# A ninth seven-product pair in the down products of a float32 encoder trunk

## The chip, the cores and the metric

The kernel runs on one core of a Trainium2 chip. The core has TensorE (PE, matrix products), VectorE (DVE), ScalarE (ACT) and GpSimd (POOL), each working off its own list of instructions in order, and SyncE (SP), which issues DMAs. The engines wait for one another by semaphores. The metric is the device time of one launch in microseconds. In the profile PEld is the loading of a weight tile into PE, which lies beside the matmuls.

## The reference

Two layers work on 256 tokens of width 2048, all in float32. Layer 0 mixes tokens with a convolution module, layer 1 with multi-head latent attention; each is followed by the same MLP, on which the change bears:

```python
h = rms_norm(x, norm_mlp_g[layer])
x = x + jnp.square(jax.nn.relu(h @ w1)) @ w2      # w1: 2048 x 8192, w2: 8192 x 2048
...
return rms_norm(x, final_norm_g)
```

## The kernel before

**Products in halves.** A float32 value is used as a sum of two rounded ones, `hi` and `lo`. A weight tile of 1 MB (two or four blocks of 128 rows) is loaded by SP into one of three `raw` buffers; ACT copies it into `hi` (the copy rounds, L170 or L497), DVE forms `lo = raw - hi` (L174 or L498). A product is then three matmuls into the same PSUM bank: hi x hi, hi x lo, lo x hi (`mm3`, L203 to L205).

**The MLP.** `mlp` (L609) cuts the 8192 hidden columns into two halves (`hf`). In each half the *up product* (L640 to L687) makes 4096 hidden columns in eight groups of four blocks: PE's products with `w1` (L655, L656), then on ACT and DVE the sum, the squared ReLU and the scaling by `r2_row` (L673 to L677), and the split of the result into `hi` and `lo`. A group holds two *pairs* of 128-row blocks; a half has 16 pairs. The *down product* (L708 to L754) multiplies these 16 pairs by `w2` in two *sweeps*, `n = 0` and `n = 2`, each over two column blocks of 512. A pair, two token tiles and two column blocks make a 2 x 2 by 2 x 2 block product.

**Two ways to do a pair.** `Sums.plain` (L559) does it with eight products, 24 matmuls. `Sums.mixed` (L546) does it with seven products (Strassen's scheme in Winograd's form), 21 matmuls. Seven products need sums of weight blocks: `mixed_weights` (L490) splits b11, b21 and b22 (1024 and 512 columns), overwrites `raw` with four differences t1 to t4 (L505, 1024 columns; L506 and L507, 512 each), and splits those too (2 x 1024). They also need sums of the inputs, which `mixed_inputs` (L512) makes during the up product: seven blocks instead of four, so more memory. `MIXED` (L44) lists the pairs that are done so: eight of 16, seven in the last half of layer 1.

**Banks and the join.** A sweep uses eight PSUM banks: four sums `e[t][c]`, one for each token tile and column block, and four shared ones, u1, u6, u7, u5. `join` (L582) adds up the shared ones after the last mixed pair, while PE does the last plain pairs, and `put` (L575) adds the results to the residual `xs`: on DVE, or, where `by_dma` holds, by an adding DMA that POOL issues (L578). `by_dma` holds in both sweeps of the first half of each layer and in the first sweep of layer 1's second half, five sweeps in all. `close` (L595) then adds the four `e`.

**What sets the order.** The code names a sequence; a list scheduler of the tile framework turns it into one fixed order for each engine, by its own estimates of when operands and buffers will be free. So a change in buffers also changes the order. Within a sweep the code interleaves mixed pairs (M) and plain ones (P) by L713: the first sweep of eight was P P MM P MM P M P MM P M P [join] P, the second P M P M P MM P M P M P MM P [join] P. Buffers: three `raw`; six of `hi` and six of `lo` of 1024 columns (`WB`), one ring for all stages in `wpool`; four `v` tiles, used for the up product's results and as room for the join.

## Time and profile before

| | |
|---|---|
| median of 3 runs | 1934.01 us (1933.93 to 1934.53) |
| the profiled execution | 1934.31 us, its span in the trace 1932.5 us |
| granted TensorE clock | 0.999 |
| layer 0: up, down, up, down | from 300.3, 478.0, 641.4 and 819 us |
| layer 1: up, down, up, down | from 1241.3, 1419.2, 1582.4 and 1760 us, to 1925 us |
| ACT busy in these down products | 91 to 93 us each |
| POOL busy over the span | 249.0 us (13%) |

The page is one execution. A row of a group reads: line, engine, operation, what is written <- what is read, shape, count | busy us, mean ns of one | idle us before them and what ended it. A row of the timeline reads: start us, length, engine, line, operation; `x2` are two in a row, and brackets tell the idle time before and who ended it. Lengths of neighbouring instructions of one engine overlap a little, so what an instruction costs in a row of many is read from one start to the next. A row of stretches gives, after the length, the busy us of PE, PEld, DVE, ACT and POOL.

### The profile page before, as it was taken

The page shows a single profiled execution, that of the slowest core. Times are in us where ns is not written, and L with a number is a line of the kernel's source. Part 1 is how long each engine was busy: PE and PEld are TensorE (multiplying, and loading weights), DVE is VectorE, ACT ScalarE, POOL GpSimd, SP SyncE. Part 2 cuts the span into 40 slices and gives each one's busy share as a digit, 9 for nine tenths or more (in the row PEclk, how much of TensorE's full clock was granted, in tenths as well). Part 3 has the DMA queues.
Part 4 walks back from the last instruction along what each step waited for, and adds up shares of the span by engine and source line. Part 5 has one row for each costly group of instructions (what it writes and reads, how often), then busy time and mean ns, then how long its engine had stood idle before and what let it go on. Part 6 is the DMA issues. An engine that isn't in the chain of part 4 may idle for free.

```text
span 1932.5 us, 28477 instructions
## 1 busy us (share of the span) xinstructions
PE 1921.0 (99%) x10725; PEld 1681.5 (87%) x10725; DVE 1592.2 (82%) x2457; ACT 1095.6 (57%) x1636; POOL 249.0 (13%) x208
## 2 busy tenths in 40 slices
PE   9999999999999999999999999999999999999998
PEld 8999888888888888888898998888888888888887
DVE  7999988877999776799976766877789987678998
ACT  5667755554555545555576655555555554455554
POOL 6999200000010100000001420000000010000000
PEclk9999999999999999999999999999999999999999
DMA  7766456665585866655656545465646776665774
GB/s 230 214 183 189 153 189 206 193 194 177 175 251 194 263 195 187 194 174 196 217 176 175 142 134 192 155 216 186 188 162 225 222 248 212 191 196 175 231 219 150
DMA packets 230427, 375.50 MB, mean 194 GB/s; under 512 B 16392, under 2 KB 107792, under 8 KB 230032
## 3 DMA queue, kind: packets, MB, share of 16 engines
q1 hardware_dynamic: 224640, 363.28, 58.7%
q0 software_dynamic: 4320, 7.87, 2.2%
q10 hardware_dynamic: 1328, 2.52, 0.4%
q8 instruction: 84, 1.38, 0.3%
q14 instruction: 55, 0.45, 0.1%
HBM read 363.68 MB, written 2.10 MB: 189 GB/s over the span
## 4 chain that ended last, share of the span: by engine, by line
PE 97%; DVE 2%; DMA 0%; ACT 0%; issue 0%; ACTq 0%; DVEq 0%
PE acc L655 24%; PE acc L205 15%; PE acc L203 15%; PE acc L204 15%; PE acc L656 13%; PE acc L823 8%; PE acc L1287 2%; DVE sum L910 1%; DMA xs<-in_x 0%; PE acc L1535 0%; PE acc L1566 0%; PE acc L1565 0%; PE acc L1536 0%; PE acc L1564 0%; PE acc L1537 0%; PE tr L267 0%
## 5 line engine op out<-in xcount | busy, mean ns | idle before, releaser
L174 DVE TENSOR_TENSOR lo<-raw,hi 128x1024 fp32r<-128x1024 f32 (+2 forms) x509 | 602.2, 1197 | 232.3 <-ACT hi L170 226.6
L170 ACT ACTIVATE hi<-raw 128x1024 fp32r<-128x1024 f32 (+2 forms) x574 | 583.9, 1036 | 361.1 <-PE acc L655 203.7
L655 PE MATMUL acc<-xt,hi 128*128 128x512 f32 x2048 | 710.6, 390 | 0.0
L656 PE MATMUL acc<-xt,lo 128*128 128x256 f32 x2048 | 577.5, 282 | 0.0
L655 PEld LDWEIGHTS acc<-xt,hi 128*128 128x128 f32 x2048 | 384.3, 188 | 80.7
L656 PEld LDWEIGHTS acc<-xt,lo 128*128 128x128 f32 x2048 | 387.1, 189 | 0.2
L497 ACT ACTIVATE hi<-raw 128x1024 fp32r<-128x1024 f32 x248 | 228.7, 948 | 228.3 <-DVE raw L505 134.0
L498 DVE TENSOR_TENSOR lo<-raw,hi 128x1024 fp32r<-128x1024 f32 x248 | 263.9, 1087 | 27.6 <-ACT hi L497 22.5
L203 PE MATMUL acc<-hi,sh 128*128 128x512 f32 x514 | 200.1, 389 | 0.0
L205 PE MATMUL acc<-lo,sh 128*128 128x512 f32 x514 | 200.1, 389 | 0.0
L203 PE MATMUL acc<-hi,gh 128*128 128x512 f32 (+1 forms) x516 | 200.0, 388 | 0.0
L205 PE MATMUL acc<-lo,gh 128*128 128x512 f32 (+1 forms) x516 | 199.9, 387 | 0.0
L204 PE MATMUL acc<-hi,gl 128*128 128x512 f32 (+1 forms) x516 | 199.9, 387 | 0.0
L823 PE MATMUL acc<-xt,hi 128*128 128x256 f32 x1024 | 180.2, 281 | 0.3 <-ACT b L1106 0.2
L204 PE MATMUL acc<-hi,sl 128*128 128x512 f32 x450 | 175.1, 389 | 0.0
L578 POOL DMA_DIRECT2D xs<-v x30 | 26.5, 994 | 1136.4 <-DVE lo L174 703.2
L910 DVE SCALAR_TENSOR_TENSOR sum<-ub,w_dw,sum 128x256 f32<-128x256 f32 x409 | 164.3, 481 | 3.6 <-ACT sum L880 3.0
L174 POOL TENSOR_TENSOR lo<-raw,hi 128x1024 fp32r<-128x1024 f32 x65 | 155.0, 2410 | 17.3 <-ACT hi L170 17.3
L823 PEld LDWEIGHTS acc<-xt,hi 128*128 128x128 f32 x1024 | 154.8, 188 | 1.1 <-ACT xt L1090 0.6
L823 PE MATMUL acc<-xt,lo 128*128 128x256 f32 x512 | 139.2, 279 | 0.0
L205 PEld LDWEIGHTS acc<-lo,sh 128*128 128x128 f32 x514 | 96.5, 188 | 20.4 <-DVE lo L498 0.3
L204 PEld LDWEIGHTS acc<-hi,gl 128*128 128x128 f32 x516 | 96.9, 188 | 19.9
(314 smaller groups left out, 2531.3 us busy)
## 6 DMA issues: line engine op xcount, KB each, us to landing
raw<-in_mlp_w SPq DMA_DIRECT2D x255, 1024.0 KB, 5.5
raw<-in_conv_w_pw SPq DMA_DIRECT2D x62, 512.0 KB, 5.1
raw<-in_conv_w_pw SPq DMA_DIRECT2D x16, 1024.0 KB, 5.1
raw<-in_mla_w_o SPq DMA_DIRECT2D x16, 1024.0 KB, 5.7
raw<-in_mla_w_kv_up SPq DMA_DIRECT2D x32, 256.0 KB, 3.9
xs<-v POOLq DMA_DIRECT2D x30, 256.0 KB, 7.8
raw<-in_mla_w_in SPq DMA_DIRECT2D x8, 576.0 KB, 3.8
raw<-in_mla_w_in SPq DMA_DIRECT2D x4, 1024.0 KB
```

Source lines behind the costliest of these rows:

```text
L170: nc.scalar.activation(hi, raw[:, js, :], AF.Copy)
L174: eng.tensor_tensor(lo, raw, hi.bitcast(F32), op=ALU.subtract)
L203: nc.tensor.matmul(ps, sh, mh, start=start, stop=False)
L204: nc.tensor.matmul(ps, sl, mh, start=False, stop=False)
L205: nc.tensor.matmul(ps, sh, ml, start=False, stop=stop)
L497: nc.scalar.activation(hi, src, AF.Copy)
L498: nc.vector.tensor_tensor(lo, src, hi.bitcast(F32), op=ALU.subtract)
L655: nc.tensor.matmul(ps[b], wh[:, bs], xhl(k), start=k == 0, stop=False)
L656: nc.tensor.matmul(ps[b][:, :S], wl[:, bs], xh(k), start=False, stop=k == KC - 1)
L823: nc.tensor.matmul(pss[c][b][:, :S], w[i][:, bs], (xh, xl)[j](k), start=k == i + j == 0, stop=end and k == k0 + nk - 1 and (i, j) == terms ...
L910: nc.vector.scalar_tensor_tensor(out=out, in0=ubs[c][:, w : w + S], scalar=tap(c, w), in1=base, op0=ALU.mult, op1=ALU.add)
L1287: nc.tensor.matmul(ps2[b][t], x_kt(k, t), w[:, bs], start=k == g == i == 0, stop=k == KC - 1 and i == len(group) - 1,)
```

## The change

A ninth pair (pair 2) is done with seven products, in all four halves; the last half has eight instead of seven. To make room for its inputs, and for the way the lower halves are now made, several things change with it:

- `mixed_weights`: b21, b22 and b11 lie side by side in `raw` and are split at once, with 1536 columns (one ACT copy and one DVE difference in place of two each). The differences are formed in another order of blocks, with the same widths, and split in two steps of 1024.
- Split buffers: `hi` and `lo` of the MLP are of two kinds, `a` (two buffers of up to 1536 columns: the first half of a plain unit, the 1536 columns of a mixed one) and `b` (three of 1024). They and those of the other stages now come from a pool that each stage opens for itself.
- `mixed_inputs`: three blocks are split in one step.
- `join` uses three rooms, not four; the first shared sum goes to `xs` by a DVE addition, never by DMA. There are three `v` tiles; `r2_row` lies in `scratch`.
- The hidden results are kept in tiles by pair, with tiles of its own for pairs 2 and 3.

```diff
-MIXED = {(layer, half): (0, 1, 4, 5, 8, 9, 12) + (13,) * (layer + half < 2) for layer in range(2) for half in range(2)}
-N_MIXED = 4
+MIXED = {(layer, half): (0, 1, 2, 4, 5, 8, 9, 12) + (13,) * (layer + half < 2) for layer in range(2) for half in range(2)}
+SPLIT_BUFS = {"a": 2, "b": 3}
...
+    def open_halves(cx, name, kinds=False):
+        halves_of[:] = [cx.enter_context(tc.tile_pool(name=name, bufs=1, reuse_waits="tile"))]
+        two_kinds[0] = kinds
+
+    def in_halves(shape, kind=None):
+        kind = kind if two_kinds[0] else None
+        n = WB if kind is None else SPLIT_BUFS[kind]
+        return [halves_of[0].tile(shape, F32R, tag=c + (kind or ""), name=nm(c), bufs=n) for c in ("hi", "lo")]
...
-        hi = wpool.tile([P, nj // 2, cols], F32R, tag="hi", name=nm("hi"), bufs=WB)
-        lo = wpool.tile([P, nj // 2, cols], F32R, tag="lo", name=nm("lo"), bufs=WB)
+        hi, lo = in_halves([P, nj // 2, cols], "ab"[h])
...
-        b11, b21 = halves(raw[:, :, :NB])
-        (b22,) = halves(raw[:, 1:2, NB:])
-        top = raw[:, 0, :].rearrange("p (c n) -> p c n", c=2)
-        low = raw[:, 1, :].rearrange("p (c n) -> p c n", c=2)
-        nc.vector.tensor_tensor(top, raw[:, :, NB:], top, op=ALU.subtract)
-        nc.vector.tensor_tensor(low[:, 1, :], low[:, 1, :], top[:, 0, :], op=ALU.subtract)
-        nc.vector.tensor_tensor(low[:, 0, :], low[:, 0, :], low[:, 1, :], op=ALU.subtract)
-        t1, t3 = halves(top)
-        t4, t2 = halves(low)
+        r = raw.rearrange("p j (c n) -> p (j c) n", c=2)
+        h1, l1 = in_halves([P, 3, NB], "a")
+        nc.scalar.activation(h1, r[:, :3, :], AF.Copy)
+        nc.vector.tensor_tensor(l1, r[:, :3, :], h1.bitcast(F32), op=ALU.subtract)
+        nc.vector.tensor_tensor(
+            r[:, 2:4, :], r[:, 3:4, :].broadcast_to([P, 2, NB]), r[:, 2:0:-1, :], op=ALU.subtract
+        )
+        nc.vector.tensor_tensor(r[:, 1, :], r[:, 1, :], r[:, 2, :], op=ALU.subtract)
+        nc.vector.tensor_tensor(r[:, 0, :], r[:, 0, :], r[:, 1, :], op=ALU.subtract)
+        b21, b22, b11 = ((h1[:, i, :], l1[:, i, :]) for i in range(3))
+        t = []
+        for i in (2, 0):
+            h2, l2 = in_halves([P, 2, NB], "b")
+            nc.scalar.activation(h2, r[:, i : i + 2, :], AF.Copy)
+            nc.vector.tensor_tensor(l2, r[:, i : i + 2, :], h2.bitcast(F32), op=ALU.subtract)
+            t += [(h2[:, j, :], l2[:, j, :]) for j in range(2)]
+        t1, t3, t4, t2 = t
...
-        halves(a[:, 0:1, :], 0, 1)
-        halves(a[:, 2:4, :], 1, 2)
+        halves(a[:, 0:3, :], 0, 3)
...
-            a, b, c, d = (room() for _ in range(4))
+            a, c, d = (room() for _ in range(3))
             nc.scalar.activation(a, u1, AF.Copy)
-            self.put(0, 0, a if self.by_dma else u1)
-            nc.vector.tensor_tensor(b, u6, a, op=ALU.add)
-            nc.vector.tensor_tensor(c, u7, b, op=ALU.add)
+            x = self.place(0, 0)
+            nc.vector.tensor_tensor(x, u1, x, op=ALU.add)
+            nc.vector.tensor_tensor(a, u6, a, op=ALU.add)
+            nc.vector.tensor_tensor(c, u7, a, op=ALU.add)
             nc.vector.tensor_tensor(d, u5, c, op=ALU.add)
-            nc.vector.tensor_tensor(b, u5, b, op=ALU.add)
-            for (t, n), o in (((1, 0), c), ((1, 1), d), ((0, 1), b)):
+            nc.vector.tensor_tensor(a, u5, a, op=ALU.add)
+            for (t, n), o in (((1, 0), c), ((1, 1), d), ((0, 1), a)):
                 self.put(t, n, o)
...
+            open_halves(cx, f"halves{layer}", kinds=True)
...
-            r2_row = mp.tile([P, S], F32, name=nm("r2_row"))
+            r2_row = scratch[:, :S]
...
-                return mp.tile([P, 2, S], F32, tag="v", name=nm("v"), bufs=4)
+                return mp.tile([P, 2, S], F32, tag="v", name=nm("v"), bufs=3)
```

The scheduler gives DVE another order. In the rows below the line numbers are those of each kernel: after the change L508 is the 1536-column lower half of a mixed pair, L509 the 1024-column difference, L512 and L513 the two of 512, L519 the lower halves of 1024, L185 those of a plain pair.

First place, DVE in the first sweep of layer 0's first down product, the end of a group of two mixed pairs and a plain one. Before, from the second mixed pair on:

```order
L498 TENSOR_TENSOR lo_5710<-raw_5707,hi_5709 128x1024
L498 TENSOR_TENSOR lo_5714<-raw_5707,hi_5713 128x512
L505 TENSOR_TENSOR raw_5707<-raw_5707 128x1024
L506 TENSOR_TENSOR raw_5707<-raw_5707 128x512
L507 TENSOR_TENSOR raw_5707<-raw_5707 128x512
L498 TENSOR_TENSOR lo_5721<-raw_5707,hi_5720 128x1024
L498 TENSOR_TENSOR lo_5725<-raw_5707,hi_5724 128x1024
L174 TENSOR_TENSOR lo_5752<-raw_5749,hi_5751 128x1024
L174 TENSOR_TENSOR lo_5756<-raw_5749,hi_5755 128x1024
```

After, from the third difference of the first mixed pair (`raw_5693`) on; `raw_5731` is the second, `raw_5769` the plain one:

```order
L513 TENSOR_TENSOR raw_5693<-raw_5693 128x512
L519 TENSOR_TENSOR lo_5703<-raw_5693,hi_5702 128x1024
L508 TENSOR_TENSOR lo_5734<-raw_5731,hi_5733 128x1536
L519 TENSOR_TENSOR lo_5707<-raw_5693,hi_5706 128x1024
L509 TENSOR_TENSOR raw_5731<-raw_5731 128x1024
L185 TENSOR_TENSOR lo_5772<-raw_5769,hi_5771 128x1024
L512 TENSOR_TENSOR raw_5731<-raw_5731 128x512
L519 TENSOR_TENSOR lo_5741<-raw_5731,hi_5740 128x1024
L513 TENSOR_TENSOR raw_5731<-raw_5731 128x512
L519 TENSOR_TENSOR lo_5745<-raw_5731,hi_5744 128x1024
L185 TENSOR_TENSOR lo_5776<-raw_5769,hi_5775 128x1024
```

What a pair's weights need was one block of rows; now the pairs are interleaved, and the last lower half of the second mixed pair follows directly on the last difference.

Second place, DVE at the end of the same sweep: the join, the closing additions (L601 before, L613 after) and the first splits of the next sweep. Before:

```order
L589 TENSOR_TENSOR v_6055<-acc_5477,v_6054 128x512
L174 TENSOR_TENSOR lo_6119<-raw_6116,hi_6118 128x1024
L590 TENSOR_TENSOR v_6056<-acc_5478,v_6055 128x512
L591 TENSOR_TENSOR v_6054<-acc_5478,v_6054 128x512
L174 TENSOR_TENSOR lo_6123<-raw_6116,hi_6122 128x1024
L498 TENSOR_TENSOR lo_6153<-raw_6150,hi_6152 128x1024
L498 TENSOR_TENSOR lo_6157<-raw_6150,hi_6156 128x512
L505 TENSOR_TENSOR raw_6150<-raw_6150 128x1024
L601 TENSOR_TENSOR xs<-acc_5471,xs 128x512
L601 TENSOR_TENSOR xs<-acc_5473,xs 128x512
```

After:

```order
L185 TENSOR_TENSOR lo_5996<-raw_5989,hi_5995 128x1024
L600 TENSOR_TENSOR v_6023<-acc_5474,v_6023 128x512
L185 TENSOR_TENSOR lo_6038<-raw_6035,hi_6037 128x1024
L601 TENSOR_TENSOR v_6024<-acc_5475,v_6023 128x512
L185 TENSOR_TENSOR lo_6042<-raw_6035,hi_6041 128x1024
L602 TENSOR_TENSOR v_6025<-acc_5476,v_6024 128x512
L603 TENSOR_TENSOR v_6023<-acc_5476,v_6023 128x512
L613 TENSOR_TENSOR xs<-acc_5469,xs 128x512
L613 TENSOR_TENSOR xs<-acc_5471,xs 128x512
L185 TENSOR_TENSOR lo_6088<-raw_6085,hi_6087 128x1024
L185 TENSOR_TENSOR lo_6092<-raw_6085,hi_6091 128x1024
L508 TENSOR_TENSOR lo_6122<-raw_6119,hi_6121 128x1536
```

The sum `c` (L589 before, `v_6024` of L601 after) and the closing addition to the same place (the second L601, the second L613) were nine rows apart with the next sweep's first splits between them; now the addition is five rows on, and the next sweep's first splits stand behind it.

Third place, DVE where the convolution module ends (residual additions L388 before, L399 after; transpositions L334, L345) and the MLP of layer 0 begins. Before:

```order
L174 TENSOR_TENSOR lo_3852<-raw_3845,hi_3851 128x1024
L174 TENSOR_TENSOR lo_3896<-raw_3893,hi_3895 128x1024
L388 TENSOR_TENSOR xs<-acc_3612,xs 128x512
L388 TENSOR_TENSOR xs<-acc_3613,xs 128x512
L334 STREAM_TRANSPOSE ca<-xs 32x2x4x32 x12
L174 TENSOR_TENSOR lo_3900<-raw_3893,hi_3899 128x1024
```

After, where `raw_3803` is the MLP's first unit:

```order
L399 TENSOR_TENSOR xs<-acc_3615,xs 128x512
L399 TENSOR_TENSOR xs<-acc_3616,xs 128x512
L345 STREAM_TRANSPOSE ca<-xs 32x2x4x32
L185 TENSOR_TENSOR lo_3806<-raw_3803,hi_3805 128x1024
L345 STREAM_TRANSPOSE ca<-xs 32x2x4x32 x2
L185 TENSOR_TENSOR lo_3810<-raw_3803,hi_3809 128x1024
```

Five splits of the MLP's first units stood ahead of the additions; now all stand behind them.

More of the change, by code (lines that the diff above doesn't have):

```diff
@@ L114, in trunk_kernel @@
     psum, psum_cx = {}, [ExitStack()]
+    halves_of, two_kinds = [], [False]
+    def open_halves(cx, name, kinds=False):
[5 more added lines that the diff above has]
+        return [halves_of[0].tile(shape, F32R, tag=c + (kind or ""), name=nm(c), bufs=n) for c in ("hi", "lo")]
     def repool(name, **banks):
@@ L490, in mixed_weights @@
     def mixed_weights(raw):
-        def halves(src):
-            hi = wpool.tile(list(src.shape), F32R, tag="hi", name=nm("hi"), bufs=WB)
-            lo = wpool.tile(list(src.shape), F32R, tag="lo", name=nm("lo"), bufs=WB)
-            nc.scalar.activation(hi, src, AF.Copy)
-            nc.vector.tensor_tensor(lo, src, hi.bitcast(F32), op=ALU.subtract)
-            return [(hi[:, i, :], lo[:, i, :]) for i in range(src.shape[1])]
-        b11, b21 = halves(raw[:, :, :NB])
-        (b22,) = halves(raw[:, 1:2, NB:])
-        top = raw[:, 0, :].rearrange("p (c n) -> p c n", c=2)
-        low = raw[:, 1, :].rearrange("p (c n) -> p c n", c=2)
-        nc.vector.tensor_tensor(top, raw[:, :, NB:], top, op=ALU.subtract)
-        nc.vector.tensor_tensor(low[:, 1, :], low[:, 1, :], top[:, 0, :], op=ALU.subtract)
-        nc.vector.tensor_tensor(low[:, 0, :], low[:, 0, :], low[:, 1, :], op=ALU.subtract)
-        t1, t3 = halves(top)
-        t4, t2 = halves(low)
+        r = raw.rearrange("p j (c n) -> p (j c) n", c=2)
[15 more added lines that the diff above has]
+        t1, t3, t4, t2 = t
         return b11, b21, b22, t1, t2, t3, t4
@@ L521, in mixed_inputs @@
         a = v.rearrange("p k (t n) -> p (k t) n", t=T)
-        a11, a21, a12, a22 = (a[:, i, :] for i in range(4))
-        halves(a[:, 0:1, :], 0, 1)
-        halves(a[:, 2:4, :], 1, 2)
+        a12, a22, a11, a21 = (a[:, i, :] for i in range(4))
+        halves(a[:, 0:3, :], 0, 3)
         nc.vector.tensor_tensor(a22, a21, a22, op=ALU.add)
-        nc.vector.tensor_tensor(a21, a11, a21, op=ALU.subtract)
+        nc.vector.tensor_tensor(a21, a21, a11, op=ALU.subtract)
         nc.vector.tensor_tensor(a11, a22, a11, op=ALU.subtract)
@@ L550, in mixed @@
             work = [
-                (u1, 0, b11), (u5, 6, t1), (u7, 4, t3), (u6, 3, t2),
-                (self.e[0][0], 1, b21), (self.e[0][1], 5, b22), (self.e[1][0], 2, t4),
+                (u1, 2, b11), (u5, 4, t1), (u7, 6, t3), (u6, 5, t2),
+                (self.e[0][0], 0, b21), (self.e[0][1], 3, b22), (self.e[1][0], 1, t4),
             ]
@@ L638, in mlp @@
                 plain = [g for g in range(ng) if g not in mixed]
-                gs = {}
+                fs = {}
                 for g in range(ng):
@@ L662, in mlp @@
                         beside = None
-                    if g in mixed or g in plain[len(plain) + len(mixed) - N_MIXED :]:
-                        shape = [P, 2, 7, P] if g in mixed else [P, 4, S]
-                        gs[g] = [mp.tile(shape, F32R, tag=f"s{c}", name=nm(f"s{c}"), bufs=N_MIXED) for c in "hl"]
-                    else:
-                        gs[g] = [mp.tile([P, 4, S], F32R, tag=f"g{c}", name=nm(f"g{c}"), bufs=ng - N_MIXED) for c in "hl"]
-                    gh, gl = gs[g]
+                    both = [2 * g, 2 * g + 1]
+                    if g % 2 == 0:
+                        tiles = [mp.tile([P, 2, 7, P], F32R, tag=f"s{c}", name=nm(f"s{c}"), bufs=ng // 2) for c in "hl"]
+                        for b2, p in enumerate(both):
+                            fs[p] = [a[:, b2] for a in tiles]
+                    elif g == 1:
+                        fs[2] = [mp.tile([P, 7, P], F32R, tag=f"o{c}", name=nm(f"o{c}")) for c in "hl"]
+                        fs[3] = [mp.tile([P, 2 * T, P], F32R, tag=f"p{c}", name=nm(f"p{c}")) for c in "hl"]
+                    else:
+                        tiles = [mp.tile([P, 2, 2 * T, P], F32R, tag=f"g{c}", name=nm(f"g{c}"), bufs=ng // 2 - 1) for c in "hl"]
+                        for b2, p in enumerate(both):
+                            fs[p] = [a[:, b2] for a in tiles]
                     for b2 in range(2):
@@ L677, in mlp @@
                         nc.vector.tensor_tensor(v, v, row, op=ALU.mult)
+                        h, l = fs[2 * g + b2]
                         if 2 * g + b2 in ms:
-                            mixed_inputs(v, gh[:, b2], gl[:, b2])
+                            mixed_inputs(v, h, l)
                             continue
-                        if g in mixed:
-                            v = v.rearrange("p k (t n) -> p (k t) n", t=T)
-                            h, l = gh[:, b2, : 2 * T, :], gl[:, b2, : 2 * T, :]
-                        else:
-                            h, l = (a[:, 2 * b2 : 2 * b2 + 2, :] for a in (gh, gl))
+                        v = v.rearrange("p k (t n) -> p (k t) n", t=T)
+                        h, l = h[:, : 2 * T, :], l[:, : 2 * T, :]
                         nc.scalar.activation(h, v, AF.Copy)
@@ L692, in at @@
                     def at(k, t):
-                        a = gs[k // 4][i]
-                        if k // 4 in mixed:
-                            return a[:, k % 4 // 2, k % 2 * T + t, :]
-                        return a[:, k % 4, t * P : (t + 1) * P]
+                        return fs[k // 2][i][:, k % 2 * T + t, :]
                     return at
@@ L703, in mixed_quad @@
                 def mixed_quad(sums, i):
-                    g, b = divmod(ms[i], 2)
-                    sums.mixed(w, k_lo + 4 * g + 2 * b, gs[g][0][:, b], gs[g][1][:, b], i == len(ms) - 1)
+                    sums.mixed(w, k_lo + 2 * ms[i], *fs[ms[i]], i == len(ms) - 1)
                 split_end = last and finish is not None
@@ L758, in trunk_kernel @@
     with ExitStack() as cx:
+        open_halves(cx, "halvesc")
         cv = cx.enter_context(tc.tile_pool(name="cv", bufs=1, reuse_waits="tile"))
@@ L1309, in rotary_tables @@
     def rotary_tables(pool):
-        place = pool.tile([P, 2, S], F32, tag="v", name=nm("v"), bufs=4).rearrange("p a n -> p (a n)")
+        place = pool.tile([P, 2, S], F32, tag="v", name=nm("v"), bufs=3).rearrange("p a n -> p (a n)")
         at = [0]
@@ L1370, in trunk_kernel @@
     with ExitStack() as cx:
+        open_halves(cx, "halvesa")
         at = cx.enter_context(tc.tile_pool(name="at", bufs=1, reuse_waits="tile"))
```

## The prediction

> **What bounds the kernel now.** I read the page's first two parts, then the busy times by stage, then the waits of PE, then PE and DVE instruction by instruction inside one down product.

> ```profile
> span 1932.5 us, 28477 instructions
> PE 1921.0 (99%) x10725; PEld 1681.5 (87%) x10725; DVE 1592.2 (82%) x2457; ACT 1095.6 (57%) x1636; POOL 249.0 (13%) x208
> ...
> PE acc L1001 <- POOL ident masks.py:199: 1.6, 1, 1.6
> PE acc L1061 <- DVE y L225: 0.6, 1, 0.6
> ...
> 300.30:478.00 177.70, 177.70 (x1027) 157.51 (x1026) 139.11 (x242) 95.47 (x140) 0.00 (x0) 1.00 0.60 190
> 478.00:641.40 163.40, 163.40 (x723) 135.32 (x722) 152.59 (x164) 92.70 (x104) 8.91 (x10) 1.00 0.65 209
> 819.00:980.00 161.00, 161.00 (x713) 133.05 (x712) 153.80 (x170) 91.14 (x109) 0.25 (x2) 1.00 0.57 190
> 1419.20:1582.40 163.20, 163.20 (x722) 135.12 (x721) 152.94 (x163) 92.68 (x104) 8.76 (x10) 1.00 0.65 209
> 1760.00:1925.00 165.00, 164.73 (x739) 136.68 (x737) 151.28 (x179) 91.60 (x116) 5.26 (x6) 1.00 0.61 198
> ```

> The last four rows are the four down products (busy us of PE, PEld, DVE, ACT and POOL after the length). PE is never idle there, and no wait of PE over 0.6 us lies outside the start. But DVE is busy 152.6 of 163.4 us: the stage that the change touches has two engines near their limit. What a matmul costs is read from starts, since the 0.39 us shown is pipelined:

> ```profile
> 640.13 0.39 PE L204 MATMUL acc<-hi,gl 128*128 128x512 f32 x1
> 640.36 0.39 PE L205 MATMUL acc<-lo,gh 128*128 128x512 f32 x1
> 640.58 0.39 PE L203 MATMUL acc<-hi,gh 128*128 128x512 f32 x1
> ```

> They start 0.22 to 0.23 us apart, and 163.4 / 723 is 0.226; I use 0.227. A plain pair (P, 24 matmuls) is 5.45 us of PE, a seven-product pair (M, 21) is 4.77.

> DVE in the first sweep of the first down product:

> ```profile
> 488.07 2.96 DVE L498 TENSOR_TENSOR lo<-raw,hi 128x1024 fp32r<-128x1024 f32 x3 [1.21 <-ACT hi L497]
> ...
> 498.24 1.82 DVE L498 TENSOR_TENSOR lo<-raw,hi 128x1024 fp32r<-128x1024 f32 x2
> ...
> 514.03 1.82 DVE L498 TENSOR_TENSOR lo<-raw,hi 128x1024 fp32r<-128x1024 f32 x2
> 515.77 1.22 DVE L505 TENSOR_TENSOR raw<-raw 128x1024 f32<-128x1024 f32 x1
> 517.02 0.69 DVE L506 TENSOR_TENSOR raw<-raw 128x512 f32<-128x512 f32 x1
> 517.75 0.69 DVE L507 TENSOR_TENSOR raw<-raw 128x512 f32<-128x512 f32 x1
> 518.36 2.52 DVE L498 TENSOR_TENSOR lo<-raw,hi 128x1024 fp32r<-128x1024 f32 x2
> 520.79 2.35 DVE L174 TENSOR_TENSOR lo<-raw,hi 128x1024 fp32r<-128x1024 f32 x2
> 523.07 1.82 DVE L498 TENSOR_TENSOR lo<-raw,hi 128x1024 fp32r<-128x1024 f32 x2
> ...
> 545.61 4.62 DVE L174 TENSOR_TENSOR lo<-raw,hi 128x1024 fp32r<-128x1024 f32 x4
> ```

> From 488 on DVE runs back to back. M takes it 520.79 - 514.03 = 6.76 us, P 2.28, M M P 514.03 - 498.24 = 15.79. So M is bound by DVE (6.76 against 4.77) and P by PE. The old sweep, P P MM P MM P M P MM P M P P, balances from its first M to the P behind its last: DVE 3 x 15.79 + 2 x 9.04 = 65.5, PE 3 x 14.98 + 2 x 10.22 = 65.4.

> **The change part by part.**

> *PE.* Eight sweeps lose three matmuls each: 24 x 0.227 = 5.4 us gained, if data is ready. The four up products prepare one more pair each; DVE has 177.7 - 139.1 = 38.6 us free there, which also covers the third tile in place of four, so 0. The loads keep their bytes.

> *Groups M M P.* The new first sweep is P P MMM P MM P MM P MM P P, the second P M P MM P MM P MM P MM P P: no M P is left in which DVE catches up. The new order of DVE (first place in the section on the change) is, for a group, S T t t s, then S' s T' P t' s t' s P', where S is the joined 1536-column difference, T the 1024-column one, t the 512-column ones, s a 1024-column lower half. Prices: 1024 columns (4.62 - 1.22) / 3 = 1.13; S between 1.13 + 0.54 (512 more columns by the two forms of L498 below) = 1.67 and the 1.74 of the two that it replaces, taken 1.67; T before a dependent t 1.25, t before t 0.73, t 0.61.

> ```profile
> L498 DVE TENSOR_TENSOR lo<-raw,hi 128x1024 fp32r<-128x1024 f32 x186 | 225.5, 1221 | 27.6 <-ACT hi L497 22.5 <-PE acc L205 0.6
> L498 DVE TENSOR_TENSOR lo<-raw,hi 128x512 fp32r<-128x512 f32 x62 | 42.4, 684 | 0.0
> L497 ACT ACTIVATE hi<-raw 128x1024 fp32r<-128x1024 f32 x186 | 195.0, 1058 | 222.3 <-DVE raw L505 134.0 <-DVE raw L507 34.5 <-PE acc L204 23.6
> L497 ACT ACTIVATE hi<-raw 128x512 fp32r<-128x512 f32 x62 | 38.4, 619 | 6.0 <-PE acc L204 5.9
> raw<-in_mlp_w SPq DMA_DIRECT2D x255, 1024.0 KB, 5.5
> ```

> S T t t s is 1.67 + 1.25 + 0.73 + 0.61 + 1.13 = 5.39. S' needs its ACT copy, 1.06 + 0.44 = 1.50 us, which ACT starts behind the copy for s, so at 5.50. Then S' 1.67, s 1.13, T' 1.13, P 1.13, t' 0.60, s 1.13, t' 0.69 bring it to 12.98. The last s needs the ACT copy of what that t' has just written; in the old order the other s stood in between, now nothing does: 1.21 idle, the price in the row at 488.07. With s and P', 1.13 each: 16.45 us, against PE's 66 x 0.227 = 14.98. There is a second limit: three buffers of loaded weights. The second M's is released by its last s, 15.3 us into the group; the load that follows takes 5.5, and its copy is wanted 4.0 us into the next group, at 20.4: 0.5 late. So a group takes 16.45 to 17.0 and PE loses 1.5 to 2.0; I take 1.8. The first group of a sweep is partly covered by DVE's lead: I take 0.5 between 0 and 1.8. Six sweeps of nine: 6 x (0.5 + 3 x 1.8) = 35. Layer 1's second half has eight: its first sweep three such groups, 3 us; its last, where units are half as wide (DVE 8 x 6.5 + 8 x 1.13 = 61 against PE (8 x 21 + 96) x 0.227 = 60), 4, between 0 and 8. Together 42, with ends of 12 (first two groups of each sweep covered, 1.0 for the others) and 65.

> *The join.* Two pieces of work change place (second place in the section on the change). Where sums go out by DMA, row (1,0) of the residual gets `c` by a POOL put, and then its plain sum by a DVE addition that must wait for that put.

> ```profile
> 550.87 0.69 DVE L589 TENSOR_TENSOR v<-acc,v 128x512 f32<-128x512 f32 x1
> ...
> 560.45 1.28 DVE L601 TENSOR_TENSOR xs<-acc,xs 128x512 f32<-128x512 f32 x2
> ...
> 552.12 0.87 POOL L578 DMA_DIRECT2D xs<-v  x1 [3.96 <-PE acc L205]
> ...
> xs<-v POOLq DMA_DIRECT2D x30, 256.0 KB, 7.8
> ...
> 642.10 0.69 DVE L601 TENSOR_TENSOR xs<-acc,xs 128x512 f32<-128x512 f32 x1 [0.50 <-DMA xs<-v]
> ...
> DMA to landing us min/median/max: 5.7/7.9/10.3
> ```

> Before, 9 us of other DVE work lie between `c` (ends 551.56) and the second L601 (561.05), POOL issues 0.56 us behind `c`, and a put lands 7.8 later (median of all; the last row is of the six around this sweep's end); even so the other sweep waits 0.50. Now only P, d, the last sum and one addition stand between, 1.13 + 3 x 0.6 = 2.9 us, so DVE waits 0.5 + 7.8 - 2.9 = 5.4 us, and behind it in DVE's order stand both halves of the next unit's weights. From the last s of the sweep: `c` ends after P, sum, P, sum = 3.5; addition possible at 11.8; next weights at 11.8 + 0.6 + 1.2 = 13.6. PE has then left 13 + 24 matmuls and some 0.7 us of handing over, 9.1. PE waits 4.5, at five ends of sweep: 22 us, with ends 0 (put landing in 2.9) and 30. The three temporaries make ACT's copies at the end wait for the same puts; they stand behind the next unit's copies and I charge nothing more. The added fourth addition (0.6) lies in the last s's wait; five puts fewer cost POOL nothing that anybody awaits.

> Where sums go by DVE (layer 0, second half), all four closing additions now stand ahead of the next weights, and the last needs the end of PE's last matmul: addition 0.6 + weights 1.22, some 2 us, twice: 4 (0 to 6).

> *Changes of stage.* Split buffers now belong to a pool of each stage. Entering layer 0's MLP, DVE used to split ahead of the residual additions, now behind (third place).

> ```profile
> 298.66 1.23 DVE L174 TENSOR_TENSOR lo<-raw,hi 128x1024 fp32r<-128x1024 f32 x1 [1.50 <-ACT hi L170]
> 299.83 1.37 DVE L388 TENSOR_TENSOR xs<-acc,xs 128x512 f32<-128x512 f32 x2
> 301.24 5.38 DVE L334 STREAM_TRANSPOSE ca<-xs 32x256 f32<-32x256 f32 x12
> ```

> The first lower half now follows two additions and one transposition (301.2 + 0.45) and ends at 302.9. PE comes to it at 300.3, where the first window above begins, and four matmuls with upper halves give it 0.9 us: 1.7 late. The same at layer 1's MLP; at attention, where three splits move behind the closing additions, 1.5: 5 in all (0 to 8).

> *Sum.* -5.4 + 42 + 22 + 4 + 5 = +68 us; the profiled execution took 1934.3 us, the median 1934.0, so 2002.

> [...]

> **Rivals.** 0.2% (3.9 us) is what a measurement here can tell from no change.
> - *Puts land in time*, groups slow: 2002 - 22 = 1980. For it: DVE's lag may delay PE too. Against: the rows at 552.12 and 642.10. [...] Chance 0.14.
> - *Groups keep up*: DVE idles less than the order says, and only join and stages cost: 1934 - 5.4 + 31 = 1960. For it: pure instruction time of a group is 15.1, almost PE's. Against: the 1.21 wait has no cover. Chance 0.15.
> - *Faster*: DVE's lead covers groups and turns, and PE alone counts: 1934 - 5.4 = 1929. It needs a group in 14.98 us, so the 1.21 wait gone and a load landing in 4, and a put in 2.9 us. Chance 0.06; no effect, 0.02.
> - *Weights late as well*: loads of 7 us in place of 5.5, as the three open units bunch them, and groups of 18: 24 x 1.2 more, 2031. Chance 0.05.

> **How the numbers follow.** The forecast has 0.58. The range leaves out the faster end and the far tail, 1950 to 2036. Faster 0.06, same 0.02, slower 0.92.

> **What would show it.** Right: PE about 8 x 3 matmuls shorter but with waits at L216 on DVE lo L519 and at ACT hi L518 in the down products, down stages of 175 us and more; DVE waiting 4 to 5 us on DMA xs<-v at the closing addition, five times; DVE's busy time in these stages above 158 us. Wrong: PE back to back in the down products, which would mean that DVE runs further ahead of PE than I count; or a put that lands within 3 us.

## The result, and the profile after

The changed kernel takes 2027.0 us (median of four runs, 2024.9 to 2028.9) against 1934.0 for the kernel before: a ratio of 1.048, 95% interval 1.046 to 1.050. It is slower, as forecast, but by 93 us and not by 68. The profiled execution has a span of 2024.4 us, 91.9 more than before. Page of the changed kernel:

```profile
span 2024.4 us, 28043 instructions
PE 1953.0 (96%) x10701; PEld 1673.4 (83%) x10701; DVE 1626.0 (80%) x2423; ACT 1099.9 (54%) x1557; POOL 244.5 (12%) x203
...
raw<-in_mlp_w SPq DMA_DIRECT2D x254, 1024.0 KB, 5.4
...
xs<-v POOLq DMA_DIRECT2D x25, 256.0 KB, 8.5
```

PE has 24 matmuls less, yet its busy time is 32 us longer: a matmul in front of a wait counts with its whole 0.39 us, and matmuls that start late (0.33 us apart behind a wait in place of 0.23) or run slowly (0.43 apart in the rows below) count as busy too. Below I therefore count from starts. The busy times by stage show where the time went (first up product, then the four down products; columns as in the prediction, with granted clock, DMA share and GB/s at the end):

```profile
300.20:479.90 179.70, 178.28 (x1027) 157.38 (x1026) 143.96 (x243) 97.98 (x136) 0.00 (x0) 1.00 0.61 194
479.90:665.30 185.40, 170.85 (x717) 133.64 (x715) 157.34 (x155) 92.37 (x88) 7.13 (x8) 0.98 0.57 179
847.10:1029.00 181.90, 170.73 (x732) 132.92 (x730) 165.85 (x172) 96.62 (x101) 0.25 (x2) 1.00 0.51 172
1469.30:1654.80 185.50, 170.06 (x716) 132.60 (x715) 157.33 (x155) 92.81 (x88) 6.96 (x8) 0.99 0.57 180
1834.90:2017.00 182.10, 171.84 (x734) 134.16 (x732) 159.74 (x177) 94.16 (x107) 4.39 (x5) 0.99 0.55 175
```

The down products take 182 to 185.5 us in place of 161 to 165 (the third row ends inside the start of attention), the up product 2 more. In them DVE is busier than before, yet idle for 16 to 28 us a stage, and the granted clock is 0.98 and 0.99 in three of the rows, where it was 1.00. What PE waits for, by line:

```profile
PE acc L214 <- ACT hi L518: 19.6, 26, 1.1
PE acc L216 <- DVE lo L185: 11.2, 3, 5.3
PE acc L214 <- ACT hi L507: 10.3, 16, 1.5
PE acc L669 <- DVE lo L185: 7.3, 4, 2.6
PE acc L216 <- DVE lo L519: 4.8, 7, 2.3
```

L507, L508, L518 and L519 are the weights of seven-product pairs, L185 those of plain pairs and of the up products. DVE's timeline shows one group M M P of the first sweep:

```profile
525.96 1.76 DVE L508 TENSOR_TENSOR lo<-raw,hi 128x1536 fp32r<-128x1536 f32 x1
...
532.16 1.76 DVE L508 TENSOR_TENSOR lo<-raw,hi 128x1536 fp32r<-128x1536 f32 x1 [0.59 <-ACT hi L507]
...
538.98 0.68 DVE L513 TENSOR_TENSOR raw<-raw 128x512 f32<-128x512 f32 x1
540.87 1.23 DVE L519 TENSOR_TENSOR lo<-raw,hi 128x1024 fp32r<-128x1024 f32 x1 [1.20 <-ACT hi L518]
542.01 1.22 DVE L185 TENSOR_TENSOR lo<-raw,hi 128x1024 fp32r<-128x1024 f32 x1
543.19 1.76 DVE L508 TENSOR_TENSOR lo<-raw,hi 128x1536 fp32r<-128x1536 f32 x1
```

The group takes 543.19 - 525.96 = 17.23 us, the one before it 16.63, with the uncovered wait of 1.20 where the forecast put it. And DVE at the end of that sweep, with its wait over all five such ends behind it:

```profile
562.44 0.68 DVE L601 TENSOR_TENSOR v<-acc,v 128x512 f32<-128x512 f32 x1
...
572.83 0.69 DVE L613 TENSOR_TENSOR xs<-acc,xs 128x512 f32<-128x512 f32 x1 [6.78 <-DMA xs<-v]
573.44 2.35 DVE L185 TENSOR_TENSOR lo<-raw,hi 128x1024 fp32r<-128x1024 f32 x2
```

```profile
DVE xs L613 <- DMA xs<-v: 24.0, 5, 6.8
```

The closing addition waits 6.78 us for the put of `c`, and the next weights stand behind it. What PE does then is new:

```profile
574.71 0.80 PE L216 MATMUL acc<-lo,ph 128*128 128x512 f32 x1 [5.27 <-DVE lo L185]
575.30 0.63 PE L214 MATMUL acc<-hi,ph 128*128 128x512 f32 x1
575.73 0.63 PE L215 MATMUL acc<-hi,pl 128*128 128x512 f32 x1
...
580.83 0.39 PE L215 MATMUL acc<-hi,pl 128*128 128x512 f32 x1
581.06 0.39 PE L216 MATMUL acc<-lo,ph 128*128 128x512 f32 x1
```

```profile
573.97:577.38 3.41, 2.67 (x6) 2.16 (x7) 3.41 (x3) 1.32 (x2) 1.45 (x2) 0.50 0.35 56
577.38:580.79 3.41, 3.41 (x9) 2.65 (x8) 2.05 (x3) 1.84 (x2) 0.32 (x1) 0.50 0.92 240
580.79:584.21 3.42, 3.42 (x16) 2.82 (x15) 2.81 (x4) 0.74 (x2) 0.00 (x0) 1.00 0.95 189
```

The last three rows are busy times by stretch: from 573.97 us on 6.8 us at a granted clock of 0.50, in which matmuls start 0.43 us apart and not 0.23, then 1.00 again. PE pays a second time for this wait: the 14 intervals from 574.71 to 580.83 us take 6.12 us, where 14 x 0.227 is 3.18.

To compare kernels I add up, from the starts of PE's matmuls behind 290 us, by how much each interval is longer than the 0.227 us of 512 columns (0.118 of 256), and sort by what ended it. "Others" are smaller delays, above all the intervals right behind a wait, where the next load of weights starts late (behind the wait of the changed kernel that ends at 540.89 us the next load starts at 540.99 and its matmul at 541.23, 0.34 behind the one before and not 0.23; 88 intervals are 0.10 to 0.15 us longer there, 1 before); of them the 7.7 us of the kernel before are taken off. The sum, less 5.4 for the 24 matmuls, gives each kernel's distance in span from before within 0.8 us (for the changed kernel 97.2 - 5.4 = 91.8 against 91.9). One thing the half-clock column misses: in eight of the kernels the clock records show one more stretch of 3.41 us at 0.50 at the start of attention (from 1009.26 us on in the run with DVE and ACT pair by pair, where the column says 0). There matmuls of 288 columns start 0.24 us apart in place of 0.13; it costs PE under 2 us.

| kernel | time, us | for weights of seven-product pairs | other waits | half clock | others |
|---|---|---|---|---|---|
| before | 1934.3 | 0 | 0 | 0 | 0 |
| changed | 2027.0 | 46.5 | 24.5 | 7.2 | 19.0 |
| eight pairs | 1984.5 | 26.1 | 7.6 | 2.1 | 14.2 |
| `c` by DVE | 2003.0 | 47.3 | 8.6 | 0.5 | 19.4 |
| DVE pair by pair | 2019.3 | 35.5 | 22.3 | 5.6 | 27.0 |
| DVE and ACT pair by pair | 1983.9 | 36.8 | 6.0 | 0 | 14.1 |
| the same, `c` by DVE | 1979.7 | 32.5 | 6.1 | 0 | 12.8 |
| nine, halves apart | 1968.9 | 19.1 | 10.9 | 0.5 | 8.8 |
| nine, apart, `c` by DVE | 1965.1 | 18.2 | 9.3 | 0 | 7.5 |
| the same, less DVE work | 1947.0 | 3.8 | 9.6 | 0.4 | 5.3 |
| the same, POOL helps | 1998.6 | 35.6 | 12.5 | 2.1 | 18.3 |
| eight, apart | 1947.5 | 0.8 | 9.5 | 0 | 1.2 |
| eight, apart, one pool | 1935.7 | 0.8 | 0.8 | 0 | 0.2 |
| the last, eight in all | 1938.9 | 4.7 | 0 | 0 | 1.5 |

### The profile page after: what moved, and what is told of

Read it like the earlier page. It is cut to its first block, busy times and chain, and to the rows that moved or that the text cites. A ratio compares the mean times of both kernels' runs of the same rounds, so it can differ in the third digit from the quotient of the medians.

```text
span 2024.4 us, 28043 instructions
## 1 busy us (share of the span) xinstructions
PE 1953.0 (96%) x10701; PEld 1673.4 (83%) x10701; DVE 1626.0 (80%) x2423; ACT 1099.9 (54%) x1557; POOL 244.5 (12%) x203
## 3 DMA queue, kind: packets, MB, share of 16 engines
q10 hardware_dynamic: 1328, 2.52, 0.4%
## 5 line engine op out<-in xcount | busy, mean ns | idle before, releaser
L181 ACT ACTIVATE hi<-raw 128x1024 fp32r<-128x1024 f32 (+2 forms) x560 | 569.8, 1033 | 413.9 <-PE acc L668 287.6
L185 DVE TENSOR_TENSOR lo<-raw,hi 128x1024 fp32r<-128x1024 f32 (+2 forms) x495 | 585.2, 1191 | 217.9 <-ACT hi L181 211.9
L518 ACT ACTIVATE hi<-raw 128x1024 fp32r<-128x1024 f32 x140 | 147.6, 1056 | 216.3 <-DVE raw L509 135.4
L214 PE MATMUL acc<-hi,sh 128*128 128x512 f32 x514 | 205.7, 404 | 31.1 <-ACT hi L518 19.4
L519 DVE TENSOR_TENSOR lo<-raw,hi 128x1024 fp32r<-128x1024 f32 x140 | 170.7, 1219 | 29.1 <-ACT hi L518 28.7
L216 PE MATMUL acc<-lo,sh 128*128 128x512 f32 x514 | 187.7, 397 | 6.1 <-DVE lo L519 4.3
L589 POOL DMA_DIRECT2D xs<-v x25 | 22.0, 978 | 1200.7 <-DVE v L601 1152.2
L214 PEld LDWEIGHTS acc<-hi,sh 128*128 128x128 f32 x514 | 96.7, 188 | 73.3 <-ACT hi L518 35.0
L185 POOL TENSOR_TENSOR lo<-raw,hi 128x1024 fp32r<-128x1024 f32 x65 | 155.0, 2411 | 17.3 <-ACT hi L181 17.3
L214 PE MATMUL acc<-hi,gh 128*128 128x512 f32 (+1 forms) x388 | 151.2, 390 | 0.9 <-ACT hi L181 0.9
L215 PE MATMUL acc<-hi,gl 128*128 128x512 f32 (+1 forms) x388 | 150.4, 388 | 0.0
L508 DVE TENSOR_TENSOR lo<-raw,hi 128x1536 fp32r<-128x1536 f32 x70 | 123.0, 1757 | 30.5 <-ACT hi L507 29.6
L216 PE MATMUL acc<-lo,gh 128*128 128x512 f32 (+1 forms) x388 | 140.4, 387 | 0.0
## 6 DMA issues: line engine op xcount, KB each, us to landing
raw<-in_mlp_w SPq DMA_DIRECT2D x254, 1024.0 KB, 5.4
raw<-in_conv_w_pw SPq DMA_DIRECT2D x16, 1024.0 KB, 5.1
raw<-in_mla_w_o SPq DMA_DIRECT2D x16, 1024.0 KB, 5.4
raw<-in_mla_w_kv_up SPq DMA_DIRECT2D x32, 256.0 KB, 4.2
xs<-v POOLq DMA_DIRECT2D x25, 256.0 KB, 8.5
raw<-in_mla_w_in SPq DMA_DIRECT2D x4, 1024.0 KB
```

Of the source, the lines that this page charges most:

```text
L181: nc.scalar.activation(hi, raw[:, js, :], AF.Copy)
L185: eng.tensor_tensor(lo, raw, hi.bitcast(F32), op=ALU.subtract)
L214: nc.tensor.matmul(ps, sh, mh, start=start, stop=False)
L215: nc.tensor.matmul(ps, sl, mh, start=False, stop=False)
L216: nc.tensor.matmul(ps, sh, ml, start=False, stop=stop)
L508: nc.vector.tensor_tensor(l1, r[:, :3, :], h1.bitcast(F32), op=ALU.subtract)
```

## The experiments

**Eight pairs.**

```
-MIXED = ... (0, 1, 2, 4, 5, 8, 9, 12) + ...
+MIXED = ... (0, 1, 4, 5, 8, 9, 12) + ...
```

> The changed kernel with the ninth pair taken back (pair 2 plain again, eight pairs in most sweeps), all else as changed. PE's waits in the changed kernel, added up by place: about 55 us in the groups M M P, 28 at the five ends of sweep with DMA puts, 7 at the two without, 4 at the changes of stage. Theory A (the new order of DVE, in which two pairs are interleaved and the last lower half waits uncovered for its ACT copy, makes a group 16.6 to 17.2 us): the three groups M M P of a sweep stay as long, but the M P between them give DVE 1 us back each, so the groups cost about 20 in place of 55; two more plain lower halves stand ahead of the waiting addition at the turn, 28 -> 15; the 24 matmuls come back, +5.4. Together 1984 us. Theory B (nine pairs are simply more work than DVE can do, in any order): with eight the groups cost nothing again, 1934 + 15 + 7 + 4 = 1960 us. If the number of pairs does not matter at all, 2015 and more.

Measured 1984.5 us, ratio to before 1.026 (1.024 to 1.027). The time is theory A's, but its parts are not, so that the fit is partly luck: the waits for seven-product weights are 26 where it had 20, all other waits 8 where it had 26, and 14 of small delays were in nobody's sum. So with the old number of pairs the rest of the change still costs 50 us.

**`c` added by DVE.**

```
     def put(self, t, c, o):
-            if self.by_dma:
+            if self.by_dma and (t, c) != (1, 0):
```

> The changed kernel, but row (1,0) of the residual gets its joined sum by a DVE addition (0.6 us) and not by a DMA put, so that the closing addition behind it has nothing to wait for. Theory C (at the five ends of sweep PE waits because DVE, with the next weights queued behind, waits for that put): the 4 to 7 us waits of DVE on DMA go, PE's 28 us at these places fall to about 5, and no stretch at half clock follows them: 2027 - 23 = 2004 us, DVE idle on DMA at L613 near 0. Rival (DVE is late there anyway, so that another wait takes the place): 2019 us and more.

Measured 2003.0 us, 1.035 (1.034 to 1.037): 24.0 less than the changed kernel, as theory C has it. Other waits fall by 15.9 and the half clock by 6.7, while the waits for seven-product weights stay as they were (46.5 and 47.3). (The columns explain 21.4 us, as the profiled executions differ by 21.1; the one of this kernel was the slowest of its four.) The put costs about a quarter of the whole loss, and nothing takes its place.

**The split as before, nine pairs.** Its weight differences keep the signs of the old split, while the inputs have those of the new, so its output isn't the reference's; every instruction has the old size.

```
-        h1, l1 = in_halves([P, 3, NB], "a")
...
+        b11, b21 = halves(raw[:, :, :NB])
+        (b22,) = halves(raw[:, 1:2, NB:])
...
-            open_halves(cx, f"halves{layer}", kinds=True)
+            open_halves(cx, f"halves{layer}")
```

> The changed kernel with nine pairs, three temporaries and the new closing, but with the split of a seven-product pair as before (1024 and 512 columns apart, one kind of six split buffers); DVE then does one pair after the other and does not interleave two. Theory A (order, not amount): a group M M P takes 2 x 6.76 + 2.28 = 15.8 us against PE's 14.98, so the groups cost 6 x (0.5 + 3 x 0.8) + 4 = 22 in place of 55, the turns some 5 less than 28: 1988 us. Theory B (amount): DVE has even 0.07 us more per pair to do, 2020 us and more.

Measured 1968.9 us, 1.018 (1.016 to 1.019), 19 less than theory A expected and 58 less than the changed kernel. Amount of work alone (theory B) can't be the main loss: this kernel has a little more of it. So the main loss is the joined half, with its two kinds of buffers and the orders that go with them; the next runs take the orders apart.

**DVE pair by pair.**

```
+                    kept = ExitStack()
+                    kept.enter_context(tc.manual_schedule(engines={mybir.EngineType.DVE}))
                     for i, k in enumerate(ks):
+                        if i == len(ks) - TAIL + 1:
+                            kept.close()
```

> The changed kernel with every instruction of it, but DVE is told to take the weights of a sweep's pairs in the order in which they are written (S T t t s s of one pair, then the next), up to the last two pairs of the sweep; the rings of split buffers and the joined lower half stay. Theory A: the last lower half is then covered by the one before it (1.13 us beside an ACT wait of 1.2), a pair takes 6.5 us of DVE and 0.2 to 0.8 of waits, a group M M P 15.7 to 16.3 us in place of 16.6 to 17.2: 55 -> 25 us, 1997 us. Theory B (amount), and a theory D that the smaller rings (two of one kind, three of the other) hold DVE back whatever its order: 2020 us and more; under D DVE's waits at L508 and L519 would end with PE, not with ACT.

Measured 2019.3 us, 1.044 (1.042 to 1.045). Only 8 less than the changed kernel, where theory A wanted 30. DVE's order was not the cause by itself. The rows of ACT and then of DVE in this run say why:

```profile
512.44 1.49 ACT L507 ACTIVATE hi<-raw 128x1536 fp32r<-128x1536 f32 x1 [4.49 <-DMA raw<-in_mlp_w]
513.83 1.99 ACT L518 ACTIVATE hi<-raw 128x1024 fp32r<-128x1024 f32 x2
```

```profile
512.84 0.69 DVE L513 TENSOR_TENSOR raw<-raw 128x512 f32<-128x512 f32 x1
514.91 2.36 DVE L519 TENSOR_TENSOR lo<-raw,hi 128x1024 fp32r<-128x1024 f32 x2 [1.37 <-ACT hi L518]
```

ACT had been given the next pair's joined copy ahead of the two copies of this pair. It stood there for a load until 512.44, though the first difference was done soon after 512, and then took 1.49 us; the copies that DVE needed came behind it. A group still takes 17.2 us. The wait ends with ACT and a load, not with PE, so theory D (rings) doesn't describe it.

**DVE and ACT pair by pair.**

```
-   engines={mybir.EngineType.DVE}
+   engines={mybir.EngineType.DVE, mybir.EngineType.Activation}
```

> As the run with DVE's pairs kept apart, and now ACT too takes the copies of a sweep's weights in the order in which they are written, so that the joined copy of the next pair no longer stands ahead of the two copies of this one (there the joined copy waited 4.5 us for its load, and the two behind it came 1.4 us late once in a group). Theory F (ACT's order was the rest of the loss): a group M M P falls from 17.2 to 15.4 us, 1995 us. Theory E (the joined copy of 1.49 us has no cover in any order: behind the last copy of a pair it runs beside one lower half of 1.13, so that DVE waits 0.4 each pair): 2 x 6.9 + 2.7 = 16.6 us a group, 2010 us. Theory D (rings): 2020 us, waits that end with PE.

Measured 1983.9 us, 1.026 (1.024 to 1.027): 35 less by ACT's order. DVE in the first sweep:

```profile
509.50 1.75 DVE L508 TENSOR_TENSOR lo<-raw,hi 128x1536 fp32r<-128x1536 f32 x1
...
525.65 1.75 DVE L508 TENSOR_TENSOR lo<-raw,hi 128x1536 fp32r<-128x1536 f32 x1
```

A group takes 16.15 us (525.65 - 509.50; the lower half of its second pair lies between), between the two expectations. The time is below both, and the table says why. The groups are the smaller part: seven-product waits and others together fall by 11.6, other waits and half clock by 21.9. With ACT in order the scheduler put one lower half of the next sweep's weights ahead of the closing addition (at 563.06 us; the addition then waits 4.34 us for the put), so PE had work while DVE waited. Neither theory had that.

**The same, with `c` by DVE.**

> The changed kernel with nothing taken back but the orders: DVE and ACT take the weights of a sweep pair by pair (1983.9 us), and row (1,0) is added by DVE. PE's waits at the ends of sweep were already down to some 6 us in all with the order alone, since more halves of weights stand ahead of the waiting addition; so 1979 us. If the put still cost what it did in the changed kernel, 1960.

Measured 1979.7 us, 1.023 (1.022 to 1.025), as expected. With weights ahead of it, the put costs 4 us and not 24: how much it costs hangs on what stands behind the addition that waits. What still lies between this and nine pairs with halves apart (1965.1) is 14.6 us of joined half and rings; part is the last sweep of all, whose order was not set, and I haven't split it further.

**Nine pairs, halves apart, `c` by DVE.** The joined half becomes one of 1024 and one of 512 columns, with one kind of six buffers, and nothing else.

> Nine pairs, the lower half taken apart again (1024 and 512 columns, one kind of six buffers), and row (1,0) added by DVE in place of the DMA put. The run with the old split took 1968.9 us; the waits for the put (8.0 us of DVE at two ends of sweep of the first down product) go. Theory C: PE gains about 2 us at each of five ends, 1959 us. If DVE is the bound there in any case, 1968. What then stays over 1934 is what nine pairs cost in groups M M P with nothing else wrong: by 15.8 against 14.98 us, about 20 us less 5.4 of matmuls, and 4 to 8 of stages.

Measured 1965.1 us, 1.016 (1.014 to 1.018), 3.8 less than the run with the old split, which has the put; nearer to the second expectation than to theory C's.

**The same, with less for DVE to do.** It leaves out the second 512-column difference of each seven-product pair, so its output isn't the reference's.

```
-        nc.vector.tensor_tensor(r[:, 0, :], r[:, 0, :], r[:, 1, :], op=ALU.subtract)
```

> The kernel with nine pairs, lower halves apart and row (1,0) added by DVE (1965.1 us), with the second 512-column difference of each seven-product pair left out, so that the output is not the reference's; PE, ACT and the loads do all that they did. DVE has 0.6 to 0.7 us less per pair. Theory B in its true form (what stays over 1934 is DVE's amount of work): a group M M P asks 14.5 us of DVE against 14.98 of PE, PE's waits for weights of such pairs (18 us) go, 1945 us. If latency behind the copies or the ring of six holds PE, 1960 us and more.

Measured 1947.0 us, 1.006 (1.005 to 1.008). The group of the kernel with all its work, and then of this one, in DVE's timelines:

```profile
509.54 1.82 DVE L511 TENSOR_TENSOR lo<-raw,hi 128x1024 fp32r<-128x1024 f32 x2
...
525.56 1.82 DVE L511 TENSOR_TENSOR lo<-raw,hi 128x1024 fp32r<-128x1024 f32 x2
```

```profile
508.03 1.82 DVE L511 TENSOR_TENSOR lo<-raw,hi 128x1024 fp32r<-128x1024 f32 x2
...
512.32 2.36 DVE L522 TENSOR_TENSOR lo<-raw,hi 128x1024 fp32r<-128x1024 f32 x2 [0.48 <-ACT hi L521]
...
523.43 1.82 DVE L511 TENSOR_TENSOR lo<-raw,hi 128x1024 fp32r<-128x1024 f32 x2
```

(In these kernels the copies and lower halves of the seven-product pairs are L510 and L511, and L521 to L523.) 16.02 us become 15.40 (part of what is saved comes back as a wait of 0.48), and the waits for these weights fall from 18.2 to 3.8 us. Leaving the difference out also shortens the chain of work behind a pair's load, but that chain is not what binds the kernel with all its work: there DVE has no idle time of 0.15 us or more from 493.55 to 563.36 us. So the ninth pair, in the best order tried, costs DVE's work: 18.1 us go with 0.6 us of it per pair, against 5.4 of matmuls gained.

**POOL for the second lower half of plain pairs.**

```
-   split(load(...), nc.vector)
+   split(load(...), nc.vector, nc.vector if end else nc.gpsimd)
```

> The last kernel, with the second lower half of each plain pair but the last of a sweep computed by POOL (2.4 us there, which has little else to do) in place of DVE. Theory B in its true form (with pairs in order, nine of them are 0.8 us a group too much for DVE): a group then asks 15.8 - 1.1 = 14.7 us of DVE against 14.98 of PE, the groups cost nothing, and 1934 - 5 + 4 (stages) + 7 (ends of sweep) = 1940 us. Rival: POOL and DVE slow one another on the same memory, lower halves of 1.13 take 1.5 and more: 1960 us and above.

Measured 1998.6 us, 1.033 (1.032 to 1.035): 33 slower than without POOL's help. DVE's lower halves of 1024 columns in the first down product, without and then with it (groups by line, mean ns behind the busy time):

```profile
L511 DVE TENSOR_TENSOR lo<-raw,hi 128x1024 fp32r<-128x1024 f32 x18 | 21.9, 1219 | 1.5 <-ACT hi L510 1.5
```

```profile
L511 DVE TENSOR_TENSOR lo<-raw,hi 128x1024 fp32r<-128x1024 f32 x18 | 34.5, 1917 | 7.6 <-ACT hi L510 7.6
```

DVE spends 12.6 us more on them, for ten lower halves of 1.13 saved, and stands idle 6.1 us longer before them. A group M M P takes 17.09 us (508.82 to 525.91) in place of 16.02: the rival holds, though no trace shows that it is the memory on which they slow one another.

**Eight pairs, halves apart.** Against "Nine pairs, halves apart", nine pairs become eight, and `c` goes out by DMA again.

> What is left of the change when the ninth pair, the joined lower half and the two kinds of buffers are taken back: three temporaries, the new closing, split buffers in a pool of each stage, the new order of the inputs. By theory A and C the groups cost nothing again (DVE 15.8 and 9.0 us for M M P and M P against PE's 15.0 and 10.2), the stages 4, the turns about 2 each at seven ends of sweep: 1934 + 4 + 14 = 1952 us. If this rest costs nothing, 1936; if it carries a loss of its own in the groups, 1965 and more.

Measured 1947.5 us, 1.007 (1.005 to 1.009). The groups cost nothing (0.8), and the ends of sweep hardly anything; what is left are waits at the changes of stage. PE's timeline at the entry of the first MLP:

```profile
302.67 0.74 PE L673 MATMUL acc<-xt,lo 128*128 128x256 f32 x4 [1.42 <-DVE lo L185]
```

**The same, with one pool.**

```
-        halves_of[:] = [cx.enter_context(tc.tile_pool(name=name, bufs=1, reuse_waits="tile"))]
+        halves_of[:] = [wpool]
```

> The kernel with eight pairs, lower halves apart, three temporaries and the new closing (1947.5 us), with the split buffers in one pool for the whole kernel again. In the trace of the 1947.5 us PE waits 1.8 us at the entry of each MLP, 2.4 in its second unit, 2.5 at the entry of attention, 0.9 at one end of sweep, and nowhere else in the down products. If the pools of the stages cause these, 1936 us; if they only cause the waits at the very entry (1.8 + 1.8 + 2.5), 1941; if it is the closing or the temporaries, 1947 as before.

Measured 1935.7 us, 1.0007 (0.9998 to 1.0016). The pools of the stages are the 11.7 us. Three temporaries, the new closing and the new order of inputs are left with 1.4 us, at most some 3.

**Eight pairs everywhere.**

> As the run with one pool, with an eighth pair in layer 1's second half too (it has seven): 6 matmuls less, 1.4 us, if DVE keeps up there. Expected 1.4 us below that run, so no more than 1.5 us from the kernel before either way; if DVE is the bound in the last sweep, whose units are half as wide, 1 to 4 us above it.

Measured 1938.9 us, 1.0023 (1.0014 to 1.0032): 3.2 above the last one for 1.4 us of matmuls saved, with 4.7 us of waits for seven-product weights in layer 1's second half. There, too, DVE is at its limit: it has no idle time of 0.15 us or more from 1848 to 1904 us, where these waits lie. No kernel tried is faster than the one before.

Taken in one order, the loss is: closing and temporaries 1.4, pools of the stages 11.7, the ninth pair 21.4 (its matmuls already taken off), joined half with two kinds of buffers 58.1 (1934.3, 1935.7, 1947.5, 1968.9, 2027.0; the fourth is the run with the old split, which also differs in the order of the differences). In another order the shares differ: with eight pairs the joined half costs 37.0 (1947.5 to 1984.5), and the ninth then 42.5.

## Why the prediction was right and where it was wrong

- **The direction and the mechanisms** held: groups bound by DVE, and a closing addition that waits for the put. Of the named signs, the waits at L518 and L519, the down products above 175 us and the five waits of DVE for `xs<-v` (4.8 us on average) are there. One is not: DVE's busy time was to be above 158 us, and two of the four stages have 157.3. PE's waits at L507, 10.3 us for the joined copy, were not among the signs.
- **Groups M M P** (forecast 42, between 12 and 65). The two groups measured took 16.63 and 17.23 us where 16.45 to 17.0 was forecast. Added up sweep by sweep, waits and the small delays behind them, the six sweeps of nine lose 48 us (forecast 35) and layer 1's second half 11 (forecast 7): some 59 in all. A group loses its length less PE's 14.98, here 1.65 and 2.25, where 1.8 was taken; in the first sweep PE's waits alone grow from group to group, 1.55, 1.87 and 2.20. Part of it is the load for the joined copy, which was to be 0.5 us late (0.4 by the forecast's own sum): ACT stands 22.4 us in 23 such waits, about 1 us each. The cause was told too narrowly, too: the step laid it on DVE's order, but with DVE in order the group stayed at 17.2, because ACT's order held it.
- **The join** (22, 0 to 30) is 24.0 by the run that takes the put away, but for two reasons of which one was not in the sum: 15.9 of waits, less than forecast, and 6.7 of half clock. The 0.7 us of handing over in its sum was an estimate that no run shows: behind the first of these waits PE's matmul starts 0.06 us after the lower half ends (574.71 and 574.65). That the number fits is partly luck.
- **Stages** (5): PE waits 1.6 and 1.3 us at the entries of the MLPs and 1.3 at that of attention, 4.2 in all, much as forecast. With halves apart the pools alone cost 11.7, since there 2.1 us of waits come behind the first units of each MLP too; what a pool costs depends on the order that it leads to.
- **Ends where sums go by DVE** (4): one wait of 0.6 us at each of the two, so the term was too high. In its place 2.5 us of waits for the weights of plain pairs in layer 1's second half were in no term.
- **Matmuls** (-5.4): 24 fewer, as counted.
- **The rivals.** "Puts land in time" falls with a median of 8.5 us, and "groups keep up" and "faster" fall. "Weights late as well" has the nearest number (2031) but not the cause: loads land in 5.4 us, not in 7, and the two groups measured do not take 18.
- **What the miss of 25 us is made of.** By the columns of the table, small delays (19.0) and half clock (7.2) come on top, while the waits are 71.0 against the 73 of the four terms. By place, the groups cost 17 more than forecast and half clock 7 more, and the ends somewhat less; so that the waits agree as a sum is luck.

## What to carry to other kernels

Price a wait of the busiest engine at more than its length: here the work behind it started late at the next load of weights (0.10 to 0.15 us, 88 times) and, where enough of a wait fell into one window of the clock (below), ran at half speed (0.43 us from start to start in place of 0.23). Before work is given to an engine that is 93% busy beside another at 100%, add up both per group and then read the order on every engine that feeds them; here ACT's order mattered as much as DVE's. Merging two operations saved under 0.1 us here (back to back, ACT took 1.47 us for the joined copy and 1.56 for the two, DVE 1.76 and 1.82), but the merged one needs all its inputs at once: a copy of 1.49 us in place of 1.06 stood in front of others and for a load (4.49 us in the run with DVE pair by pair).

## What the runs showed of the hardware

```profile
666.13:669.54 3.41, 1.32 (x8) 1.20 (x9) 3.20 (x4) 1.54 (x2) 0.00 (x0) 1.00 1.06 274
669.54:672.95 3.41, 3.41 (x12) 2.92 (x12) 2.31 (x3) 2.99 (x4) 0.76 (x2) 0.50 1.00 251
1655.99:1659.40 3.41, 1.86 (x11) 1.66 (x12) 3.41 (x4) 1.23 (x2) 0.00 (x0) 1.00 1.09 255
1659.40:1662.81 3.41, 3.41 (x21) 3.06 (x20) 2.16 (x3) 3.38 (x4) 1.24 (x2) 1.00 0.88 259
```

In the first, PE is idle for 2.09 us of a wait of 2.57, and the window behind it runs at 0.50. In the third it is idle for 1.55 us, since its wait of 2.33 began in the window before, and the clock stays at 1.00. In the changed kernel half clock follows the windows with 2.09, 2.27, 2.29, 2.94 and 3.41 us idle, and not those with 1.87 or less. All fourteen traces, cut into such windows from 20 us on, say the same: half clock follows every window at full clock in which PE was idle for 1.9 us or more, four of the six with 1.70 to 1.88, and none with less. So what counts is not a wait's length alone. Half clock followed all six waits of 2.57 us and more, two of four between 2.1 and 2.4 (2.17 and 2.27, but neither 2.12 nor 2.33), and five of the 22 of 1.2 to 2.0 us (1.48 to 1.97, all at the start of attention). So an idle share of little more than half (1.9 of 3.41 us) was enough here.
- **POOL's lower halves held DVE's up.** One lower half on POOL took 2.7 us in the run where POOL helps. Beside one of them (507.92 to 510.61 us) DVE's two lower halves of L511, begun at 508.82, take 3.46 us; the next two, with POOL idle, take 1.82. Over the first down product one of DVE's 1024-column lower halves at L511 takes 1.9 us on average in place of 1.2.
